# Gated delta rule in one encoder layer: state updates of the two directions as neighbouring 64-row products

## The chip, the cores and the metric

The kernel runs on one core of one Trainium2 chip. The metric is the device time of one execution in microseconds (us); of several runs the median is given. Engines are named as in the profile: PE is TensorE (PEld its weight loads), DVE is VectorE, ACT is ScalarE, POOL is GpSimd, SP is SyncE, which here only issues DMAs. PSUM is the memory into which TensorE writes; it is divided into 8 banks of 512 fp32 numbers per partition.

## The reference

One layer of a bidirectional encoder over 1024 tokens of width 1024: one input projection feeds neighbourhood attention (8 heads of 64) and a gated DeltaNet (4 heads of 128, both directions), then come an output projection and a hierarchical mixture of experts. The change touches the DeltaNet's recurrence alone. Per head and direction it goes over 16 chunks of 64 tokens:

```
def step(state, inp):
    q_c, k_c, u_c, w_c, g_c, qk_c = inp
    v_new = u_c - einsum('bhck,bhkv->bhcv', w_c, state)
    o_c = (einsum('bhck,bhkv->bhcv', q_c * exp(g_c)[..., None], state)
           + einsum('bhij,bhjv->bhiv', qk_c, v_new))
    g_last = g_c[..., -1:]
    state = (state * exp(g_last)[..., None]
             + einsum('bhck,bhcv->bhkv', k_c * exp(g_last - g_c)[..., None], v_new))
    return state, o_c
```

The state is 128 x 128 per head and direction. The second direction goes over the tokens from the end.

## The kernel before

All of it is one function, `tile_layer`. Its parts in time: the projections for the DeltaNet with their convolutions and decays (to about 217 us), the inversion of the chunks' triangular matrices (lines 443 to 493, to about 351 us), the recurrence (lines 498 to 571, 360 to 513 us), the attention (from line 596), output projection and router, and the experts (from 780 us), whose weights come from HBM.

**Recurrence.** The two directions of a chunk are handled together: direction 0 has partitions 0 to 63 (`hf[0]`), direction 1 has 64 to 127 (`hf[1]`); `DH` is 4 heads, `DD` is 128, `CH` is 64, `NCH` is 16. For each chunk n:

- SP issues eight DMAs (lines 516 to 520) for the inverted matrix and the attention matrix of the chunk (`at`, block-diagonal over the two directions, zeroed once at line 507), for v (`vn`) and for k (`kn`). GpSimd scales k into `kd` (line 522).
- Line 531: TensorE multiplies k and q of the chunk (`qkT`, 128 columns: 64 of k, 64 of q) with the state, per head and direction, into the bank `pk0` or `pk1`. Lines 533: VectorE reads the k half of it into `r`, 64 rows at a time.
- Line 537: per head, one product over all 128 partitions gives the new values of both directions in the bank `pw`.
- Lines 539 and 540: after each pair of heads ScalarE copies the rows of direction 0 and VectorE those of direction 1 into `w`, in which each direction has its own 128 columns and the rest is zero (memset once at line 508, two buffers). Line 542: ScalarE copies `pw` once more as a whole into `wc`.
- Line 548: per head, one product of `kd` (all 128 partitions) with `w` (256 columns) gives the updates of both directions side by side, in the bank `ps0` for heads 0 and 1 and `ps2` for heads 2 and 3. GpSimd scales the old state (line 552), VectorE adds (line 555): `sn`, the next chunk's `st`.
- Line 560: ScalarE scales the q half of `pk` into `o`, 64 rows at a time. Line 563: per head, one product of `at` with `wc` goes into the bank of `pw`; VectorE adds it (line 567), and GpSimd issues two DMAs to `on_d` (line 569).

An fp32 product stands in the trace as two records, each with its own weight load. Each of the tiles pk0, pk1, pw, ps0 and ps2 has one bank and one buffer; three more banks (`psF`) hold the projections' results.

**What fills the gaps.** The projections of z, v, k and q of the attention (`nat_block`, lines 575 to 587; eight blocks of 192 products of 256 columns, fp32r, through `mm3` on lines 84 to 86, tile `pA`) stand behind the recurrence in the program. Each product in `mm3` is three: high parts, and high with low parts in both ways. Line 417 transposes their results on TensorE, lines 424 and 428 write k and q to DRAM (`kk_d`, `q_d`). Seven blocks are free to run beside the recurrence, and the last is mixed with the first attention steps (lines 681 to 690).

**Order.** The program is a sequence of instructions; when it is built, a scheduler puts them in an order for each engine by their places in the program and by its own estimates of times, and adds the waits. It lets two accesses to one PSUM bank not overlap, where one is a write or where two engines read. On the chip each engine then keeps its order. After the recurrence `scn.close()` and `lng.close()` (lines 592 and 593) give its memory back, and the attention's tiles are allocated in it: `vw` (line 601), loaded by 16 DMAs on SP (line 605), and the buffers for q and k (`q2`, `k2`, `kl`), loaded by DMAs that GpSimd issues (lines 620 to 622) and read on lines 639 and 640.

Of the kernel before, what the change touches and what calls it, by code (L numbers as in the profile page):

```python
# [8 lines left out]
F32 = mybir.dt.float32  # L9
# [3 lines left out]
AF = mybir.ActivationFunctionType  # L13
OP = mybir.AluOpType
# [5 lines left out]
P = 128  # L20
# [5 lines left out]
DH, DD = 4, 128  # L26
# [10 lines left out]
def tile_layer(ctx, tc, a, out):  # L37
    nc = tc.nc
    pe, act, dve, pool, sp = nc.tensor, nc.scalar, nc.vector, nc.gpsimd, nc.sync
# [24 lines left out]
    qkT = dnp.tile([P, DH, NCH, 2 * CH], F32, name="qkT")  # L64
# [110 lines left out]
    step = lambda d, n: n if d == 0 else NCH - 1 - n  # L175
    gt = dnp.tile([P, 10, NCH, DH], F32, name="gt")
    X, T1, T2, BETA, G, GC, EGC, DL, C1, C2 = (gt[:, i] for i in range(10))
    egl = dnp.tile([P, 2, NCH, DH], F32, name="egl")
# [285 lines left out]
    with tc.tile_pool(name="ty", bufs=1, side="right") as ty:  # L464
# [13 lines left out]
        for g in range(4):  # L478
            ms = range(g * 16, g * 16 + 16)
            gs = slice(g * 16, g * 16 + 16)  # L480
            pw = psB.tile([P, 16, 32], F32, name="pB")
# [17 lines left out]
    sc1 = scn.enter_context(tc.tile_pool(name="sc1", bufs=1, side="right"))  # L499
    sc2 = scn.enter_context(tc.tile_pool(name="sc2", bufs=2, side="right"))  # L500
    psK = scn.enter_context(tc.tile_pool(name="psK", bufs=1, space=PSUM, side="right"))
    hf = [slice(d * 64, d * 64 + 64) for d in range(2)]

    atb = [sc1.tile([P, 2, DH, 2, CH], F32, name=f"at{i}") for i in range(2)]
    wb = [sc1.tile([P, DH, 2, DD], F32, name=f"w{i}") for i in range(2)]
    for i in range(2):
        pool.memset(atb[i], 0.0)
        pool.memset(wb[i], 0.0)
    st = None
    for n in range(NCH):  # L510
        ch = [slice(step(d, n) * CH, step(d, n) * CH + CH) for d in range(2)]
        kn = sc2.tile([P, DH, DD], F32, name="kn")
        vn = sc2.tile([P, DH, DD], F32, name="vn")
        at, w = atb[n % 2], wb[n % 2]
        for d in range(2):
            sp.dma_start(at[hf[d], 1, :, d], T_d[hf[d], n])
            sp.dma_start(vn[hf[d]], v_d[ch[d]])
        for d in range(2):
            sp.dma_start(kn[hf[d]], k_d[ch[d]])
            sp.dma_start(at[hf[d], 0, :, d], SA_d[hf[d], n, :, 1])  # L520
        kd = sc2.tile([P, DH, DD], F32, name="kd")
        pool.tensor_tensor(kd, kn, DL[:, n, :, None].to_broadcast([P, DH, DD]), op=OP.mult)
        if n == 0:
            r = vn
        else:
            r = sc2.tile([P, DH, DD], F32, name="r")

            pk = [psK.tile([P, DH, DD], F32, name=f"pk{d}") for d in range(2)]
            for h in range(DH):
                for d in range(2):  # L530
                    pe.matmul(pk[d][:, h], qkT[:, h, step(d, n)], st[:, h, d], start=True, stop=True)
                for d in range(2):
                    dve.scalar_tensor_tensor(r[hf[d], h], pk[d][hf[0], h], nE[hf[d], n, h:h + 1], vn[hf[d], h],
                                             op0=OP.mult, op1=OP.add)
        pw = psK.tile([P, DH, DD], F32, name="pw")
        for h in range(DH):
            pe.matmul(pw[:, h], at[:, 1, h], r[:, h], start=True, stop=True)
            if h % 2 == 1:
                act.activation(w[hf[0], h - 1:h + 1, 0], pw[hf[0], h - 1:h + 1], AF.Copy)
                dve.tensor_copy(w[hf[1], h - 1:h + 1, 1], pw[hf[1], h - 1:h + 1])  # L540
        wc = sc2.tile([P, DH, DD], F32, name="wc")
        act.activation(wc, pw, AF.Copy)
        if n < NCH - 1:
            sn = sc2.tile([P, DH, 2, DD], F32, name="sn")
            for g in range(0, DH, 2):
                ps = psK.tile([P, 2, 2, DD], F32, name=f"ps{g}")
                for h in range(g, g + 2):
                    pe.matmul(ps[:, h - g], kd[:, h], w[:, h], start=True, stop=True)
                if n == 0:
                    dve.tensor_copy(sn[:, g:g + 2], ps)  # L550
                else:
                    pool.tensor_tensor(sn[:, g:g + 2], st[:, g:g + 2],
                                       egl[:, :, n, g:g + 2].rearrange("p d h -> p h d")[:, :, :, None].to_broadcast([P, 2, 2, DD]),
                                       op=OP.mult)
                    dve.tensor_tensor(sn[:, g:g + 2], ps, sn[:, g:g + 2], op=OP.add)
        o = sc2.tile([P, DH, DD], F32, name="o")
        if n > 0:
            for h in range(DH):
                for d in range(2):
                    act.activation(o[hf[d], h], pk[d][hf[1], h], AF.Copy, scale=EGC[hf[d], n, h:h + 1])  # L560
        po = psK.tile([P, DH, DD], F32, name="pw")
        for h in range(DH):
            pe.matmul(po[:, h], at[:, 0, h].rearrange("p d c -> p (d c)"), wc[:, h], start=True, stop=True)
        if n == 0:
            dve.tensor_copy(o, po)
        else:
            dve.tensor_tensor(o, po, o, op=OP.add)
        for d in range(2):
            pool.dma_start(on_d[d, ch[d]], o[hf[d]].rearrange("p h e -> p (h e)"))
        if n < NCH - 1:  # L570
            st = sn
# [362 lines left out]
    for i in range(done, nb + 3):  # L934
# [11 lines left out]
        if i >= nb // 2 + 7 and i % 2 == 0 and not (tail[0][0] is ao_pre and tail[0][1] == 4):  # L946
            f, t = tail.pop(0)
# [6 lines left out]
    def load_w(mw, e, eng=sp, after=None, how=mybir.DependencyClass.Sync, parts=(0, 1)):  # L954
        ws = []
        for i in parts:
            w = mw.tile([P, 2048], F32, name="wd") if i else mw.tile([P, 2, 2048], F32, name="wg")
            ins = eng.dma_start(w, a[("w_gu", "w_down")[i]][e])
            if after is not None:
                tc.add_manual_dep(ins.ins, after.ins.name, mybir.DependencyInfo(how, mybir.DependencyReason.DATA),  # L960
                                  reason="more urgent transfers first")
            ws.append(w)
        return ws
# [181 lines left out]
    for i in range(NS):  # L1145
        gp, e = steps[i]
        args = (pool, ins, mybir.DependencyClass.NoSync) if i == 0 else ()
        for n, part in upto(i):
            f = steps[n // 2][1]
# [20 lines left out]
    with tc.If(rest > 0):  # L1170
        with tc.For_i(0, 64) as e:
            left = nc.values_load(ci[:, bass.ds(e + 64, 1)], min_val=0, max_val=14)
            with tc.For_i(0, left) as i:
                w = load_w(mwA, e)
# [71 lines left out]
```

## Time and profile before

| | us |
|---|---|
| median of 3 runs | 1406.26 |
| lowest and highest | 1401.35 and 1408.34 |
| the profiled execution | 1408.78 |
| its span, first to last instruction | 1407.0 |
| PE busy | 1194.1 (85%) |
| DVE busy | 660.1 (47%) |
| ACT busy | 393.9 (28%) |
| POOL busy | 387.4 (28%) |

The rows below come from the profiled execution, with times from the start of its span. Busy time counts an engine while an instruction of its own runs. Matmuls are pipelined, and their ends are modelled, so a row of PE is better read by its starts: the distance from one start to the next. Idle time of an engine is put down to what released it, as the semaphores tell. The granted clock is a share of TensorE's full 2.4 GHz. The DMA share is the mean busy share of the core's 16 DMA engines, as the packets' times sum up, and can exceed 1.

### The profile page before, as it was taken

To read this page: it belongs to the slowest core of one execution; us is meant where nothing else is said; L and a number is where in the kernel's file an instruction comes from. 1 tells how busy PE (TensorE), PEld (TensorE's weight loads), DVE (VectorE), ACT (ScalarE), POOL (GpSimd) and SP (SyncE) were. 2 spreads that over 40 slices of the span, in tenths; PEclk is the share of its full clock that TensorE was granted. 3 is DMA by queue.
4 is the path that set the end of the run, shared out by engine and by line. 5 is a ranking of instruction groups with operands and counts; after the bars stand their busy time and mean duration, and the time that the engine had idled before them with its cause. 6 is when DMAs were issued, how large, how long until landed. Compare 5 with 4: busy or idle time off the path is not lost. (4 is left out here: it accounts for less than half of the span.)

```text
span 1407.0 us, 20840 instructions
## 1 busy us (share of the span) xinstructions
PE 1194.1 (85%) x7307; PEld 828.0 (59%) x7308; DVE 660.1 (47%) x1631; ACT 393.9 (28%) x800; POOL 387.4 (28%) x435
## 2 busy tenths in 40 slices
PE   6977999979999996688989968888887788878885
PEld 6866889969988895466768853333332333333332
DVE  5556853853667652667858871212211212222211
ACT  6435422322354441765445320000000000000000
POOL 1147313021655544112110242212212112211111
PEclk9989999989999997799999979999998899989998
DMA  4251246346565469998694788999999899998991
GB/s 158 71 114 42 75 135 177 94 138 148 166 176 148 119 172 221 297 262 206 169 216 165 285 332 323 397 404 401 400 406 394 352 387 407 395 364 331 402 379 38
DMA packets 109953, 347.11 MB, mean 247 GB/s; under 512 B 43104, under 2 KB 49248, under 8 KB 93168
## 3 DMA queue, kind: packets, MB, share of 16 engines
q1 hardware_dynamic: 74480, 260.68, 51.3%
q0 software_dynamic: 27056, 68.79, 19.0%
q10 hardware_dynamic: 8272, 15.78, 3.2%
q8 instruction: 82, 1.34, 0.4%
q14 instruction: 63, 0.52, 0.1%
HBM read 305.26 MB, written 61.67 MB: 261 GB/s over the span
## 5 line engine op out<-in xcount | busy, mean ns | idle before, releaser
L1041 PE MATMUL pp<-wg,xT 128*64 128x512 f32 x1024 | 233.1, 604 | 19.7 <-DVE xT L1030 19.4
L1041 PEld LDWEIGHTS pp<-wg,xT 128*64 128x64 f32 x1024 | 74.4, 139 | 156.4 <-issue 128.2
L1076 PE MATMUL po<-wd,hT 128*64 128x512 f32 x512 | 126.8, 622 | 45.1 <-DVEq L1155 28.3
L84 PE MATMUL pA<-w_hi,h_hi 128*128 128x256 f32 x512 | 151.1, 295 | 0.0
L86 PE MATMUL pA<-w_hi,h_lo 128*128 128x256 f32 x512 | 149.9, 293 | 0.0
L85 PE MATMUL pA<-w_lo,h_hi 128*128 128x256 f32 x512 | 149.9, 293 | 0.0
L1057 POOL DMA_INDIRECT out<-yg,tS x32 | 50.8, 1587 | 291.3 <-DVE yg L1078 242.8
L1045 DVE SCALAR_TENSOR_TENSOR sg<-pp,tS,sg 128x256 f32<-128x256 f32 x32 | 15.5, 484 | 233.2 <-ACTq L1155 189.0
L1076 PEld LDWEIGHTS po<-wd,hT 128*64 128x64 f32 x512 | 42.1, 142 | 129.5 <-issue 68.4
L1078 DVE TENSOR_SCALAR yg<-po,tS 128x512 f32<-128x512 f32 x64 | 47.0, 749 | 126.2 <-DMA out<-yg,tS 66.8
L84 PEld LDWEIGHTS pA<-w_hi,h_hi 128*128 128x128 f32 x512 | 100.5, 196 | 0.7 <-issue 0.2
L85 PEld LDWEIGHTS pA<-w_lo,h_hi 128*128 128x128 f32 x512 | 100.4, 196 | 0.2
L86 PEld LDWEIGHTS pA<-w_hi,h_lo 128*128 128x128 f32 x512 | 100.2, 196 | 0.3
L1044 ACT ACTIVATE sg<-pp,tS 128x256 f32<-128x256 f32 x32 | 15.2, 474 | 272.7 <-PE pp L1041 272.7
L84 PE MATMUL pA<-h_hi,w_hi 128*128 128x512 f32 x192 | 76.5, 398 | 0.0
L85 PE MATMUL pA<-h_lo,w_hi 128*128 128x512 f32 x192 | 76.4, 398 | 0.0
L86 PE MATMUL pA<-h_hi,w_lo 128*128 128x512 f32 x192 | 75.9, 395 | 0.0
L76 DVE TENSOR_TENSOR w_lo<-w_raw,w_hi 128x512 fp32r<-128x512 f32 x56 | 38.5, 702 | 71.1 <-ACT w_hi L75 69.4
L250 DVE SCALAR_TENSOR_TENSOR acc<-raw,convw,acc 128x1024 f32<-128x1024 f32 x48 | 63.2, 1320 | 12.4 <-ACT acc L248 11.9
L1053 ACT ACTIVATE hT<-ph 128x256 f32<-128x256 f32 x32 | 12.3, 384 | 191.6 <-PE ph L1051 191.6
L84 PE MATMUL pA<-wo_hi,t_hi 128*128 128x512 f32 x128 | 54.7, 427 | 9.3 <-ACT t_hi L750 6.9
L665 PE MATMUL pv<-pT,vw 128*128 128x256 f32 x192 | 55.2, 425 | 3.3 <-ACT pT L656 2.2
(340 smaller groups left out, 2422.4 us busy)
## 6 DMA issues: line engine op xcount, KB each, us to landing
wg<-in_w_gu SPq DMA_DIRECT2D x62, 2048.0 KB
wd<-in_w_down SPq DMA_DIRECT2D x63, 1024.0 KB
bt<-in_bias SPq DMA_DIRECT2D x24, 384.0 KB
w_raw<-in_w_nat SPq DMA_DIRECT2D x32, 256.0 KB
w_raw<-in_w_dn SPq DMA_DIRECT2D x24, 256.0 KB
k<-kk_d POOLq DMA_DIRECT2D x16, 384.0 KB
SA_d<-cm POOLq DMA_DIRECT2D x8, 512.0 KB
kk_d<-ev POOLq DMA_DIRECT2D x8, 512.0 KB
```

What stands on the lines that cost most here:

```text
L76: dve.tensor_sub(lo[:, k:k + 2], raw, hi[:, k:k + 2].bitcast(F32))
L84: pe.matmul(dst, sh, mh, start=(i == 0), stop=False)
L85: pe.matmul(dst, sh, ml, start=False, stop=False)
L86: pe.matmul(dst, sl, mh, start=False, stop=(i == n - 1))
L250: dve.scalar_tensor_tensor(acc, raw[:, t:t + S], convw[:, m, t:t + 1], acc, op0=OP.mult, op1=OP.add)
L665: pe.matmul(pv, vw[:, w, half + g, pr * P:(pr + 1) * P], pT[:, g], start=(g == 0), stop=(g == 2))
L1041: pe.matmul(pp[d * CAP:(d + 1) * CAP], xT[:, k, d * CAP:(d + 1) * CAP], ws[d][0][:, :, k * 256:(k + 1) * 256], start=(k == 0), stop=(k == ...
L1044: act.activation(sg[:n], pp[:n, 0], AF.Silu, scale=mf[:n, 3:4])
L1045: dve.scalar_tensor_tensor(sg[:n], pp[:n, 1], mf[:n, 3:4], sg[:n], op0=OP.mult, op1=OP.mult)
L1057: ins = pool.indirect_dma_start(out=out, out_offset=bass.IndirectOffsetOnAxis(ap=idx, axis=0), in_=yg, in_offset=None, bounds_check=S - 1, ...
L1076: pe.matmul(po[d * CAP:(d + 1) * CAP], hT[:, k, d * CAP:(d + 1) * CAP], w[1][:, k * D + c * 512:k * D + (c + 1) * 512], start=(k == 0), st ...
L1078: dve.tensor_scalar(yg[:n, cs], po[:n], mf[:n, 2:3], None, op0=OP.mult)
```

## The change

It has four parts. `w` with its zeros and its memsets goes; `pw` is copied once into `wc`, heads 0 and 1 by ScalarE and heads 2 and 3 by VectorE, after all four products. The state products are one per head and direction, over the 64 partitions of that direction, into a bank per direction; neighbours in the program are the two directions of a head. State, update and scaling are laid out by direction first, so an add takes all heads of one direction. And pk is made for all heads of direction 0, then of direction 1, each followed by VectorE's four reads.

```diff
     atb = [sc1.tile([P, 2, DH, 2, CH], F32, name=f"at{i}") for i in range(2)]
-    wb = [sc1.tile([P, DH, 2, DD], F32, name=f"w{i}") for i in range(2)]
     for i in range(2):
         pool.memset(atb[i], 0.0)
-        pool.memset(wb[i], 0.0)
...
-            for h in range(DH):
-                for d in range(2):
-                    pe.matmul(pk[d][:, h], qkT[:, h, step(d, n)], st[:, h, d], start=True, stop=True)
-                for d in range(2):
+            for d in range(2):
+                for h in range(DH):
+                    pe.matmul(pk[d][:, h], qkT[:, h, step(d, n)], st[:, d, h], start=True, stop=True)
+                for h in range(DH):
                     dve.scalar_tensor_tensor(r[hf[d], h], pk[d][hf[0], h], nE[hf[d], n, h:h + 1], vn[hf[d], h],
                                              op0=OP.mult, op1=OP.add)
         pw = psK.tile([P, DH, DD], F32, name="pw")
+        wc = sc2.tile([P, DH, DD], F32, name="wc")
         for h in range(DH):
             pe.matmul(pw[:, h], at[:, 1, h], r[:, h], start=True, stop=True)
-            if h % 2 == 1:
-                act.activation(w[hf[0], h - 1:h + 1, 0], pw[hf[0], h - 1:h + 1], AF.Copy)
-                dve.tensor_copy(w[hf[1], h - 1:h + 1, 1], pw[hf[1], h - 1:h + 1])
-        wc = sc2.tile([P, DH, DD], F32, name="wc")
-        act.activation(wc, pw, AF.Copy)
+        act.activation(wc[:, 0:2], pw[:, 0:2], AF.Copy)
+        dve.tensor_copy(wc[:, 2:4], pw[:, 2:4])
         if n < NCH - 1:
-            sn = sc2.tile([P, DH, 2, DD], F32, name="sn")
-            for g in range(0, DH, 2):
-                ps = psK.tile([P, 2, 2, DD], F32, name=f"ps{g}")
-                for h in range(g, g + 2):
-                    pe.matmul(ps[:, h - g], kd[:, h], w[:, h], start=True, stop=True)
+            sn = sc2.tile([P, 2, DH, DD], F32, name="sn")
+
+            ps = [psK.tile([P, DH, DD], F32, name=f"ps{d}") for d in range(2)]
+            for h in range(DH):
+                for d in range(2):
+                    pe.matmul(ps[d][:, h], kd[hf[d], h], wc[hf[d], h], start=True, stop=True)
+            for d in range(2):
                 if n == 0:
-                    dve.tensor_copy(sn[:, g:g + 2], ps)
+                    dve.tensor_copy(sn[:, d], ps[d])
                 else:
-                    pool.tensor_tensor(sn[:, g:g + 2], st[:, g:g + 2],
-                                       egl[:, :, n, g:g + 2].rearrange("p d h -> p h d")[:, :, :, None].to_broadcast([P, 2, 2, DD]),
-                                       op=OP.mult)
-                    dve.tensor_tensor(sn[:, g:g + 2], ps, sn[:, g:g + 2], op=OP.add)
+                    pool.tensor_tensor(sn[:, d], st[:, d], egl[:, d, n, :, None].to_broadcast([P, DH, DD]), op=OP.mult)
+                    dve.tensor_tensor(sn[:, d], ps[d], sn[:, d], op=OP.add)
```

## Rows read from the trace of the kernel before

**Rows 1.** Busy us by stretch: PE, PEld, DVE, ACT, POOL; clock, DMA share, GB/s.

```profile
366.00:512.00 146.00, 136.15 (x953) 121.25 (x953) 100.27 (x226) 69.92 (x184) 78.95 (x87) 1.00 0.53 141
...
512.00:537.00 25.00, 24.29 (x203) 23.96 (x203) 9.33 (x17) 5.01 (x9) 16.56 (x18) 1.00 1.09 281
```

**Rows 2.** Groups by line, 360 to 510 us: busy us, mean ns | idle before, releasers.

```profile
L533 DVE SCALAR_TENSOR_TENSOR r<-pk,nE,vn 64x128 f32<-64x128 f32 x120 | 41.2, 343 | 9.5 <-PE pk L531 7.0
L560 ACT ACTIVATE o<-pk,gt 64x128 f32<-64x128 f32 x117 | 37.8, 360 | 16.8 <-DVE r L533 14.9 <-ACT w L539 0.8
L86 PE MATMUL pA<-w_hi,h_lo 128*128 128x256 f32 x115 | 35.4, 308 | 0.0
...
L548 PE MATMUL ps<-w,kd 128*128 128x256 f32 x120 | 33.5, 385 | 0.5 <-DVE w L540 0.2
...
L555 DVE TENSOR_TENSOR sn<-ps,sn 128x512 f32<-128x512 f32 x28 | 19.3, 691 | 14.4 <-PE ps L548 12.8 <-PE pA L417 1.4
...
L539 ACT ACTIVATE w<-pw 64x256 f32<-64x256 f32 x32 | 12.1, 377 | 51.2 <-PE pw L537 45.4 <-DVE qn L406 5.5
```

**Rows 3.** TensorE in order of time, one chunk: start, duration, line, tiles, records.

```profile
374.30 1.03 PE L548 MATMUL ps<-w,kd 128*128 128x256 f32 x4
375.17 1.05 PE L563 MATMUL pw<-wc,at 128*128 128x128 f32 x8
376.06 0.61 PE L531 MATMUL pk<-sn,qkT 128*128 128x128 f32 x4
...
376.62 0.28 PE L85 MATMUL pA<-w_lo,h_hi 128*128 128x256 f32 x1
376.74 0.28 PE L86 MATMUL pA<-w_hi,h_lo 128*128 128x256 f32 x1
```

**Rows 4.** TensorE in order of time: products on two column halves (128*64) of the array.

```profile
211.70 1.03 PE L261 MATMUL pB<-ident,acc 128*128 128x128 f32 x8
212.67 3.71 PE L342 MATMUL pB<-qkT 128*64 128x128 f32 x64
216.31 0.38 PE L84 MATMUL pA<-w_hi,h_hi 128*128 128x256 f32 x1
```

**Rows 5.** TensorE in order of time: 32 x 32 products on different rows and columns.

```profile
349.24 0.19 PE L490 MATMUL pB<-TT,wt 32*32 32x32 f32 x1
349.25 0.19 PE L489 MATMUL pB<-TT,wt 32*32 32x32 f32 x1
349.27 0.19 PE L490 MATMUL pB<-TT,wt 32*32 32x32 f32 x1
```

**Rows 6.** Waits from 366 to 512 us: who for whom, us in total, times, longest.

```profile
PEld pk L531 <- DVE r L533: 7.5, 9, 1.4
DVE w L540 <- ACT w L539: 7.3, 6, 1.7
...
PE pk L531 <- DVE r L533: 5.6, 7, 1.2
```

**Rows 7.** All engines in order of time: from a chunk's first pk to the next.

```profile
401.64 0.68 PE L531 MATMUL pk<-sn,qkT 128*128 128x128 f32 x4
...
409.06 0.72 DVE L533 SCALAR_TENSOR_TENSOR r<-pk,nE,vn 64x128 f32<-64x128 f32 x2
...
411.52 0.43 DVE L540 COPY w<-pw 64x256 f32<-64x256 f32 x1
...
412.35 0.49 PE L531 MATMUL pk<-sn,qkT 128*128 128x128 f32 x2 [0.52 <-ACT o L560]
```

**Rows 8.** Line 508's memsets: count, duration ns min/median/max, first and last start.

```profile
L508 POOL MEMSET w<- x2: 963/970/976, 355.9 to 357.7; 128x1024 f32 x2
```

**Rows 9.** SP's issues for vw; TensorE's first attention products, with their waits.

```profile
510.48 13.30 SPq L605 DMA_DIRECT2D vw<-av_d x16
...
541.34 0.66 PE L639 MATMUL pq<-k,q 128*128 128x384 f32 x1 [4.26 <-DMA k<-kk_d]
543.60 0.66 PE L640 MATMUL pq<-kl,q 128*128 128x384 f32 x1 [1.60 <-DMA kl<-kk_d]
```

More of the change, by code (lines that the diff above doesn't have):

```diff
@@ L513, in tile_layer @@
         vn = sc2.tile([P, DH, DD], F32, name="vn")
-        at, w = atb[n % 2], wb[n % 2]
+        at = atb[n % 2]
         for d in range(2):
```

## Prediction, made before the change was built

> **What bounds the kernel now.** I read the busy time by stretch first, then the groups by line in the stretch of the recurrence, then TensorE's order in time, then the waits. The recurrence runs from 366 to 512 us: 15 chunks after the first, 9.7 us each. In it TensorE is busy 136 of 146 us at the full granted clock (1.00 in the row), VectorE 100, ScalarE 70; from 512 to 537 TensorE is busy 24.3 of 25 [rows 1]. TensorE has two kinds of work there [rows 2]: the products of the recurrence (fp32; each shows as two records) and the projection products pA (fp32r, 3 lines of 115 records), which fill the gaps; what of them doesn't fit follows until 537. So any TensorE time freed between 366 and 537 should bring the end of the projections forward, and a shorter chain of chunks alone only moves pA from inside the recurrence to behind it.
>
> How full TensorE is, its starts show better than its busy time [rows 3]: the 4 records of L548 (256 columns) take 374.30 to 375.17, 0.217 us each; the 8 of L563 (128 columns) 375.17 to 376.06, 0.111 each; pA 0.12 each. Per chunk that is 16 x 0.111 for pk, 8 x 0.111 for pw, 8 x 0.217 for the state products, 8 x 0.111 for po, and 23 x 0.12 for pA: 1.8 + 0.9 + 1.7 + 0.9 + 2.8 = 8.1 of 9.7 us. The 1.6 us that are left are waits, 24 us over 15 chunks.
>
> **The state products.** Now 4 fp32 products per chunk, 128 rows by 256 columns, half of them zeros of w: 15 x 8 x 0.217 = 26.0 us. After: 8 products of 64 rows by 128 columns, the two directions of a head next to each other on different rows of the array and in different banks. If neighbours run at the same time, the nearest rows give the price: L342, fp32 on two halves of the array, has 64 records of 128 columns from 212.67 to 216.31, 0.057 each, where L261 on the whole array takes about 0.11 [rows 4]. Then 15 x 16 x 0.057 = 13.7 us, a gain of 12.3. But L342's halves are columns of the array; a pair on different rows is only seen with 32 x 32 products, which start 0.01 us apart and come at about 0.015 us a record [rows 5]. If neighbours don't overlap, the cost is 15 x 16 x 0.111 = 26.6, a loss of 0.6. A gain beyond 12.3 is excluded: there are only two halves. I take 12.3, since L342 has the very columns and type.
>
> Going between the whole array and halves has a price. L261's 8 records should end at 211.70 + 0.89 = 212.59, and L342 starts at 212.67: 0.08 us on the way in [rows 4]. The way out I can't separate, and set equal. The two copies of pw end one after the other, so the products come in two visits a chunk: 0.2 x 2 x 15 = 6 us at most, 0 at least (one visit that coincides with a wait). I take 6. By this row the products give 12.3 - 6 = 6.3 us net.
>
> The Trainium skill speaks here against the change: TensorEngine Tiling (Array Packing), Key Properties, says that changing the tiling mode (not just the tile) drains TensorE. By that rule, with an estimate of a drain as an L548 record's duration less its pitch (0.385 less 0.217 [rows 2, 3]), two visits of two edges would cost 10 us over 15 chunks and leave 2. The trace agrees that there is a cost, but its one edge has 0.08.
>
> **The order of pk.** Now each head's two products are followed by VectorE's two reads of the same banks (0.34 us each [rows 2]), and the next head's products wait for them: 7.5 us on the weight queue, 5.6 on TensorE [rows 6]. After, four products of direction 0 run, then four of direction 1 while VectorE reads the first bank. Most of these 13.1 us should go, but something is late next: the first pk of a chunk needs the old pk read out by ScalarE's 8 scalings (0.36 us each [rows 2]; the wait at 412.35 is for them [rows 7]), and pw needs VectorE's last reads. Bounds: 13 gained, 3 lost if the new single wait is longer than the four old ones. I take 4, nearer the small end, since TensorE's order is fixed at build time and fill placed by a plan doesn't move into a wait.
>
> **Copies, adds, scalings.** Per chunk ScalarE loses one 64-row copy (0.38) and half of the whole-bank copy, VectorE one copy of 0.43 [rows 2, 7]. ScalarE and VectorE have idle time for it [rows 1], so as work this is worth nothing; if ScalarE's cover failed it would be its 0.38 a chunk. On the path the two copies still stand one behind the other (VectorE's waits on ScalarE's, 7.3 us [rows 6], although they read other partitions of the bank), 0.8 us now and then. The adds (0.69 [rows 2]) and GpSimd's scalings keep count and size: 0. The two memsets of w go, 0.97 each on GpSimd ahead of the first chunk [rows 8]; bound 0 to 1.9 us gained, taken as 0, since the first chunk also needs its DMAs. GpSimd's later instructions and the DMA issues on SP keep their places: no DMA is added or moved.
>
> **Behind the recurrence.** The attention's buffers reuse the recurrence's memory, so the 16 loads of vw are issued only from 510.48 us, over 13.3 us; DMA is then at 1.09 of its 16 engines [rows 1, 9]. In that crowd TensorE waits 4.26 us for k and 1.60 for kl [rows 9]. If the recurrence ends earlier than the projections do, these loads are out of the way. Bounds 0 to 5.9 gained; I take 4.
>
> **The sum.** 12.3 - 6 + 4 + 0 + 4 = 14.3 us. The profiled execution took 1408.8 us (span 1407.0 and 1.8 around it): 1394.5. It was 2.5 above the median of the runs shown (1406.26), so against the median 1392.0. What comes behind (attention, experts) starts on what was computed before it, so I let the gain pass through whole.
>
> **Rivals.**
> *No gain that shows.* A record of 128 stationary columns never came faster than 0.111 us [rows 3]; L342's 0.057 has 64 stationary columns [rows 4]. So it may be the weights that set the pitch, and the change has twice as many loads of 128 columns. Then the products lose 0.6 and the switches 6, against 4 and 0 to 4 gained: 0 to 3 us off, 1403 to 1409. The same follows if other work gets between the neighbours in TensorE's order. For it: the two rows can't be told apart. Against: the 32 x 32 pairs, at 0.015 a record [rows 5]. The Trainium skill has the rule, in TensorE: Matmul & The Clock Gate, LDWEIGHTS: the time of a load goes with its columns and not with its rows. No run here shows a 64-row load of 128 columns.
>
> *A larger gain.* In one chunk the first pk starts at 401.64, VectorE's last two reads end at 409.78, and the next chunk's first pk at 412.35 [rows 7]: the reads take 8.2 us of 10.7. In the new order eight reads (2.7) follow four products (0.9): near 4. The chunk could fall to some 7.5 us and the recurrence end by 480. TensorE's sum still holds, so the gain is 12.3 with switches hidden in waits, plus 11 of the 13.1 us of waits, plus 5 of DMA waits: 28 us, 1378. Against it: pA's products stand between in a fixed order, and much of the 8.2 us is pA.
>
> *Slower.* Now the first pair of heads is copied, multiplied and added while the second pair is still read; after, everything waits for the last pw, and the first pk of the next chunk stands behind pw 0.45 (two records and a tail), copies 0.38 and 0.43, products 0.6 to 1.0 and an add 0.69: 2.6 to 3.0 us, with some 0.05 at each of five hand-overs near 3.3, against 2.57 now (409.78 to 412.35) [rows 7]. If the reads keep their 8.2 us because fill stands between them, each chunk is 0.7 us longer: 15 x 0.7 = 10.5, 1417 from the median. It decides as soon as the reads take over 7.5 us.
>
> **How the numbers follow.** Forecast 0.42 (own range 1385 to 1399), larger gain 0.18, no gain 0.26, slower 0.14. Half a per cent, 7 us, is about what a measurement of this kernel can tell from no change. The first two are faster by more: 0.60; same 0.26; slower 0.14. The range for 8 in 10 leaves out most of the slower case and the far end of the larger gain: 1374 to 1411.
>
> **What would show it.** Right: the new L548 line with 240 records whose neighbours start within 0.02 us and come at 0.06 a record; the waits of pk for r nearly gone; the recurrence shorter than 140 us; TensorE's waits for k and kl under 3 us. Wrong: state records at 0.11 us, or single visits with 0.2 us around each; a longer chunk with TensorE waiting at the first pk or at pw; or a recurrence that is shorter by 10 us and more while attention starts at the same time, which would mean that something other than TensorE sets the start of attention.

## The result, and the profile after

The changed kernel takes **1387.21 us** (median of 4 runs, 1385.71 to 1392.52), where the kernel before, timed beside it, took 1407.3: a ratio of 0.9869, 95% interval [0.9842, 0.9895], 20 us less. The prediction was 1392.0, with a range of 1374 to 1411, and faster. A second measurement of the changed kernel, among the experiments, gave 1386.0 and 0.986 [0.9843, 0.9878].

Where the time went shows in four starts that every trace has: the first pk of the recurrence, the first product of the last projection block (`nat_block` number 8), VectorE's first logits, the last value product of the attention. The table gives the first, then the stretches between them, for all the kernels that follow (one profiled execution each; the two of the changed kernel show how far such numbers move by themselves).

| kernel | first pk at | to the last projection block | to the first logits | to the last values | to the end | span |
|---|---|---|---|---|---|---|
| before | 366.1 | 152.2 | 42.6 | 216.6 | 629.5 | 1407.0 |
| after | 366.0 | 138.9 | 41.2 | 215.1 | 625.2 | 1386.4 |
| after, second profile | 362.8 | 135.3 | 41.3 | 212.6 | 629.2 | 1381.2 |
| pk's order alone | 368.0 | 147.7 | 41.1 | 215.5 | 627.5 | 1399.8 |
| all but pk's order | 365.3 | 146.2 | 40.7 | 217.1 | 630.8 | 1400.1 |
| products not neighbours | 369.1 | 141.4 | 35.2 | 214.6 | 628.1 | 1388.4 |
| products on 128 rows | 368.3 | 140.6 | 40.1 | 211.5 | 630.6 | 1391.1 |
| copies back | 368.1 | 138.3 | 38.7 | 208.8 | 627.9 | 1381.8 |
| vw later | 363.8 | 135.0 | 22.4 | 223.3 | 626.7 | 1371.2 |
| vw later, second profile | 367.3 | 135.8 | 22.7 | 223.9 | 627.3 | 1377.0 |
| vw later, not neighbours | 368.2 | 139.1 | 24.6 | 227.7 | 628.8 | 1388.4 |
| vw and q, k, kl later | 368.6 | 136.3 | 22.4 | 225.7 | 628.1 | 1381.1 |
| vw in two parts | 368.7 | 136.6 | 22.7 | 228.6 | 625.1 | 1381.7 |
| a quarter of vw | 367.7 | 135.5 | 20.4 | 219.3 | 629.9 | 1372.8 |

Of the 20.6 us between the spans of before and after, 13.3 lie in the first stretch; of the 25.8 to the second profile, 16.9.

The busy time by stretch of the changed kernel (columns as in [rows 1]) covers the recurrence, which now ends at 486 us instead of 513, what follows of the projections, and the pause before the attention:

```profile
360.00:487.00 127.00, 114.63 (x1014) 108.71 (x1013) 85.69 (x212) 53.72 (x156) 74.19 (x84) 0.96 0.60 159
487.00:525.00 38.00, 36.43 (x303) 35.88 (x301) 12.88 (x24) 6.91 (x12) 21.46 (x23) 1.00 1.13 272
525.00:547.00 22.00, 11.32 (x65) 10.74 (x66) 7.32 (x23) 2.55 (x4) 10.80 (x15) 0.69 0.61 132
```

TensorE is still nearly full up to 525. But the projections that no longer fit into the shorter recurrence now run beside the DMAs, whose share rises to 1.13, and from 525 TensorE is idle half the time.

The groups by line, 360 to 500 us (columns as in [rows 2]):

```profile
L545 PE MATMUL ps<-wc,kd 64*128 64x128 f32 x240 | 18.2, 287 | 6.4 <-ACT wc L537 3.2 <-DVE wc L538 2.4 <-POOL kd L520 0.7
L529 PE MATMUL pk<-sn,qkT 128*128 128x128 f32 x240 | 32.8, 295 | 5.4 <-DVE sn L551 5.4
L531 DVE SCALAR_TENSOR_TENSOR r<-pk,nE,vn 64x128 f32<-64x128 f32 x120 | 33.7, 340 | 4.0 <-PE pk L529 2.7
```

L545 holds the new state products: 18.2 us busy instead of 33.5 for L548 [rows 2], by starts 19.6 instead of 26.7. VectorE's reads of pk (L531) keep their 340 ns, but are busy 33.7 instead of 41.2 in sum [rows 2], since eight in a row overlap. In the waits, 360 to 500 us (columns as in [rows 6]), pk no longer waits for r; it waits for the new state, and the state products for the copies:

```profile
DVE wc L538 <- ACT wc L537: 14.2, 12, 2.2
...
PEld pk L529 <- DVE sn L551: 6.3, 4, 3.5
PE pk L529 <- DVE sn L551: 5.4, 4, 3.2
...
PE ps L545 <- ACT wc L537: 3.2, 2, 2.2
PE ps L545 <- DVE wc L538: 2.4, 2, 1.5
```

One chunk, all engines in order of time (start, duration, engine, line):

```profile
424.53 1.95 PE L529 MATMUL pk<-sn,qkT 128*128 128x128 f32 x16
...
425.63 2.28 DVE L531 SCALAR_TENSOR_TENSOR r<-pk,nE,vn 64x128 f32<-64x128 f32 x8
...
428.69 0.38 ACT L537 ACTIVATE wc<-pw 128x256 f32<-128x256 f32 x1
...
429.11 0.42 DVE L538 COPY wc<-pw 128x256 f32<-128x256 f32 x1 [1.20 <-ACT wc L537]
429.22 1.16 PE L545 MATMUL ps<-wc,kd 64*128 64x128 f32 x16
...
430.31 1.16 PE L559 MATMUL pw<-wc,at 128*128 128x128 f32 x8
430.49 1.29 DVE L551 TENSOR_TENSOR sn<-ps,sn 128x512 f32<-128x512 f32 x2 [0.95 <-PE ps L545]
...
431.31 1.98 PE L529 MATMUL pk<-sn,qkT 128*128 128x128 f32 x16
```

From pk to pk it is 6.8 us (10.7 in the chunk of [rows 7]; over all chunks some 8.0 instead of 9.7). All 16 records of the state products go in one visit, a stay of TensorE on one kind of product, of 1.09 us. In single starts the two directions of a head begin 6 to 7 ns apart here (up to 36 in other visits), a pair comes every 0.112, 0.056 a record, and the last one is 0.202 before the next line's, where records on the whole array are 0.111 apart.

### The profile page after: what moved, and what is told of

It reads as the page before. It is cut to its first block, busy times and chain, and to the rows that moved or that the text cites. A ratio compares the mean times of both kernels' runs of the same rounds, so it can differ in the third digit from the quotient of the medians.

```text
span 1386.4 us, 21032 instructions
## 1 busy us (share of the span) xinstructions
PE 1177.5 (85%) x7427; PEld 821.7 (59%) x7428; DVE 643.5 (46%) x1615; ACT 375.8 (27%) x768; POOL 381.9 (28%) x433
## 5 line engine op out<-in xcount | busy, mean ns | idle before, releaser
L1037 PE MATMUL pp<-wg,xT 128*64 128x512 f32 x1024 | 229.7, 598 | 17.7 <-DVE xT L1026 16.7
L85 PE MATMUL pA<-w_lo,h_hi 128*128 128x256 f32 x512 | 148.9, 291 | 0.0
L85 PEld LDWEIGHTS pA<-w_lo,h_hi 128*128 128x128 f32 x512 | 100.9, 197 | 0.0
L85 PE MATMUL pA<-h_lo,w_hi 128*128 128x512 f32 x192 | 76.6, 399 | 0.0
L250 DVE SCALAR_TENSOR_TENSOR acc<-raw,convw,acc 128x1024 f32<-128x1024 f32 x48 | 63.2, 1319 | 11.5 <-ACT acc L248 11.1
L1049 ACT ACTIVATE hT<-ph 128x256 f32<-128x256 f32 x32 | 12.3, 384 | 193.4 <-PE ph L1047 193.4
```

Of the source, the lines that this page charges most:

```text
L85: pe.matmul(dst, sh, ml, start=False, stop=False)
L250: dve.scalar_tensor_tensor(acc, raw[:, t:t + S], convw[:, m, t:t + 1], acc, op0=OP.mult, op1=OP.add)
L1037: pe.matmul(pp[d * CAP:(d + 1) * CAP], xT[:, k, d * CAP:(d + 1) * CAP], ws[d][0][:, :, k * 256:(k + 1) * 256], start=(k == 0), stop=(k == ...
```

## The experiments

### pk's order, alone and taken back

The kernel before with the new order of pk alone, and the changed kernel with the old order:

```diff
-            for h in range(DH):
-                for d in range(2):
+            for d in range(2):
+                for h in range(DH):
                     pe.matmul(pk[d][:, h], ...
```

> The kernel before, with the new order of pk alone (four products of direction 0, VectorE's four reads, then direction 1); w, its copies and the 256-column state products stay. Theory: the waits for r go (13 us), the chunk falls from 9.7 to 8.5 to 9.0, the time is 1394 to 1401. Rival 'order alone': 1385 to 1391. Rival 'pairs alone': 1403 to 1409.

> The changed kernel, with pk's order back: per head both directions, then VectorE's two reads. Theory (the pairs save TensorE time and the order of pk shortens the chunk, both count): the state products still take about 1.0 us a chunk for 16 records, TensorE's waits for r come back (10 us and more), a chunk is 8.8 to 9.3 us, the time 1394 to 1400. Rival 'order alone': 1402 to 1409, as before the change. Rival 'pairs alone': 1385 to 1390, as with the whole change.

Measured: alone 1399.37 (1397.8 to 1401.5), 0.9953 [0.9934, 0.9971]; taken back 1397.05 (1395.1 to 1401.8), 0.9935 [0.9917, 0.9953]. So the order is worth some 6.5 us by itself and 10 on top of the products. The groups of pk's products, first in the kernel before with the new order:

```profile
L531 PE MATMUL pk<-sn,qkT 128*128 128x128 f32 x240 | 29.3, 275 | 0.0
```

then in the changed kernel with the old order (224 of the 240 records lie in the rows' window):

```profile
L529 PE MATMUL pk<-sn,qkT 128*128 128x128 f32 x224 | 46.2, 296 | 7.8 <-DVE r L531 3.9 <-DVE sn L551 3.8
```

In the old order each head's results must be read before the next head may write, so the 240 records stand in 119 short rows with fill between them; in the new one they stand in 15 rows of 16. The busy sums, 46.2 against 29.3 to 32.8, make too much of that: the last record of each row counts its whole 0.275 us, though the next product starts 0.03 to 0.11 behind it, so each further row adds to the sum without costing that time. The starts are safer. From the start before to its own, pk's 240 records take 47.9 us in the old order, 9.9 of them idle, and 36.4 in the changed kernel, 5.4 idle. So of the 11.5 us between them 4.5 show as idle; the other 7 are switches between fill and pk and short waits, which the profile counts as busy. A part of it comes back in the fill; the first stretch of the table is 7.3 us shorter. In the kernel before the new order takes pk from 45.0 us to 26.8, but TensorE's idle time ahead of pw and the state products rises from 0.8 to 11.6 us: most of the wait moves to the next step, and 4.5 us are left in the stretch.

### The products: apart, and on all rows

In the changed kernel, first the four products of direction 0, then those of direction 1:

```diff
-            for h in range(DH):
-                for d in range(2):
+            for d in range(2):
+                for h in range(DH):
                     pe.matmul(ps[d][:, h], kd[hf[d], h], wc[hf[d], h], start=True, stop=True)
```

> The changed kernel, with the eight state products ordered by direction: four of direction 0, then four of direction 1, so that neighbours stand on the same rows. Theory: the 16 records come at 0.11 us, 1.8 us a chunk in place of 1.0, which is on the chunk's path and on TensorE: 0.75 x 15 = 11 us more at most, 1394 to 1399. Rival 'order alone' (the pairing is worth nothing): 1385 to 1390. Rival 'pairs alone': 1403 and more.

And each product over 128 rows, which adds up the updates of both directions in each:

```diff
-                    pe.matmul(ps[d][:, h], kd[hf[d], h], wc[hf[d], h], start=True, stop=True)
+                    pe.matmul(ps[d][:, h], kd[:, h], wc[:, h], start=True, stop=True)
```

> The changed kernel, with the eight state products over all 128 partitions (kd[:, h], wc[:, h]), so that both banks get the sum of both directions' updates: same count, columns, banks and order, no halves of the array and no change of its division. Theory: 16 records at 0.11 us as without neighbours, but no 0.1 to 0.2 us at the edges: 1391 to 1398. If the edges cost nothing, the same as with the products ordered by direction; if they are a drain of 0.2 us each, 3 to 6 us less than that.

TensorE in order of time, products apart:

```profile
433.47 1.71 PE L545 MATMUL ps<-wc,kd 64*128 64x128 f32 x16
435.11 1.16 PE L559 MATMUL pw<-wc,at 128*128 128x128 f32 x8
```

and on 128 rows:

```profile
432.27 2.02 PE L545 MATMUL ps<-wc,kd 128*128 128x128 f32 x16
434.13 1.06 PE L559 MATMUL pw<-wc,at 128*128 128x128 f32 x8
```

The visit takes 1.64 us apart and 1.86 on 128 rows, against 1.09 as neighbours: the pairing is worth 0.55 us a chunk. Apart, the records of one direction come at 0.112, as those of 128 rows do; around the change of direction three pairs start 4 to 6 ns apart. So the 16 starts take 1.44 us, against 1.75 on 128 rows and 0.89 as neighbours.

The way out of the 64-row products costs 0.19 us more than on 128 rows: the first record of the next line comes 0.202 behind the last of theirs (0.112 on 128 rows), and its second another 0.213 behind (0.112). The rows of L559 above show the second part, 1.16 long and 1.06. The way in costs 0.08 where nothing else holds the visit: in the three visits behind a product of L85 it is 0.21 on 64 rows and 0.13 on 128. In the others both start 0.19 or more behind the last projection product, on 128 rows as soon as the copy is released.

The whole time is another matter. Apart: 1386.96 (1385.0 to 1390.2), 0.9864 [0.9844, 0.9884], the same as the changed kernel, where 1394 to 1399 was expected. On 128 rows: 1392.42 (1390.7 to 1394.9), 0.9908 [0.9888, 0.9928]. The table shows where the first loses the difference: the last projection block begins later (141.4 us after the first pk, against 135.3 and 138.9), and then 35.2 instead of 41 us pass to the first logits. What the pairing wins, the stretch before the attention takes back; with the loads of vw later, below, it shows.

### Two copies back

A ScalarE copy of the whole bank and a VectorE copy of half of it, into a tile that nobody reads:

```diff
         dve.tensor_copy(wc[:, 2:4], pw[:, 2:4])
+        wx = sc2.tile([P, DH, DD], F32, name="wx")
+        act.activation(wx, pw, AF.Copy)
+        dve.tensor_copy(wx[:, 2:4], pw[:, 2:4])
```

> The changed kernel with two copies more per chunk, into a tile that nobody reads: the whole bank by ScalarE (0.6 us) and half of it by VectorE (0.42), about what the change took off these engines. The prediction gave the copies as work no price: within 2 us of the changed kernel, chunk unchanged at 6.8 us. Rival (the copies are a part of the gain, since ScalarE's scalings, which free pk, stand behind them): a chunk 0.4 to 1.0 us longer, 1391 to 1398.

1384.98 (1382.8 to 1389.2), 0.9869 [0.9832, 0.9907]: nothing. As work the copies have no price: 16.2 us of work came in, beside TensorE's (groups by line, 360 to 500 us):

```profile
L540 ACT ACTIVATE wx<-pw 128x512 f32<-128x512 f32 x16 | 9.5, 596 | 1.4 <-DVE wc L538 1.1
L541 DVE COPY wx<-pw 128x256 f32<-128x256 f32 x16 | 6.7, 422 | 7.6 <-ACT wx L540 7.6
```

But no product reads `wx`. In the kernel before, the product behind the state products (L563) read what ScalarE's second copy wrote, and waited for it (columns as in [rows 6]):

```profile
PEld pw L563 <- ACT wc L542: 5.2, 10, 0.9
...
PE pw L563 <- ACT wc L542: 2.0, 6, 0.6
```

TensorE's 2.0 us of this are gone in the changed kernel. This run doesn't bring them back, and no other shows what they are worth in the whole time.

### What holds the stretch before the attention

In the changed kernel SP issues the loads of vw as soon as the recurrence's memory is free, and ScalarE, which splits the projections' k and q into `ev` (L421), must wait for an earlier `ev` to reach DRAM. SP's issues:

```profile
486.73 13.20 SPq L601 DMA_DIRECT2D vw<-av_d  x16
```

ScalarE in order of time:

```profile
513.65 0.69 ACT L421 ACTIVATE ev<-pA,qkg 128x512 fp32r<-128x512 f32 x1 [2.13 <-DMA kk_d<-ev]
...
523.40 0.69 ACT L421 ACTIVATE ev<-pA,qkg 128x512 fp32r<-128x512 f32 x1 [5.69 <-DMA kk_d<-ev]
```

and TensorE's pauses. The first stands behind that wait; the second is the chain of the block's last tile through ScalarE, VectorE and GpSimd, in which no wait for a DMA shows:

```profile
527.63 1.09 PE L417 MATMUL pA<-ident,qn 128*128 128x128 f32 x4 [3.37 <-DVE qn L406]
...
543.55 1.11 PE L417 MATMUL pA<-ident,qn 128*128 128x128 f32 x4 [5.92 <-DVE qn L406]
```

After the first pause TensorE's granted clock is 0.50, the lower of its two levels (1.2 GHz), for five us:

```profile
524.00:528.00 4.00, 0.63 (x5) 0.46 (x4) 2.03 (x4) 0.69 (x2) 2.89 (x3) 0.79 0.99 234
528.00:533.00 5.00, 5.00 (x23) 5.00 (x22) 0.91 (x3) 0.69 (x1) 1.97 (x3) 0.50 0.88 186
```

Columns as in [rows 1]. Four versions put transfers later; all are the changed kernel otherwise. The loads of vw wait for the last product of projection block 7:

```diff
+        for tp, _ in enumerate(nat_block(bi)):
+            if (bi, tp) == (6, 3):
+                mark = marks[tp]
...
-            sp.dma_start(vw[r * 32:(r + 1) * 32, w], src)
+            ld = sp.dma_start(vw[r * 32:(r + 1) * 32, w], src)
+            tc.add_manual_dep(ld.ins, mark.ins.name, ..., reason="later")
```

> The changed kernel, with one more wait: the 16 loads of vw wait for the last product of the seventh projection block (about 504 us), in place of the end of the recurrence (486). Theory now (behind the recurrence not TensorE binds but the ev buffers, whose writes to kk_d and q_d crawl among vw's loads): the wait of TensorE for qn near 527 us (3.4 us) goes, the first logits come 2 to 5 us earlier, 1382 to 1386. Rival (the crowd moves with the loads, or vw is then late for its first use at 552 us): 1387 to 1394, with a new wait at the first product with vw. Rival (TensorE's order alone sets the start of attention): within 2 us of the changed kernel.

The same with the products apart:

> Both edits: state products ordered by direction, so that neighbours share rows, and vw's loads behind the seventh block. If the pairs' 0.5 us a chunk was hidden by the DMA crowd, it shows once the crowd is gone: 4 to 7 us slower than with the loads later alone. If it is hidden by something else (the last block's own chain), the two are within 2 us.

vw later, and the loads of q, k and kl issued 4 steps ahead instead of 8; and with the second half of vw behind the first logits besides:

> The changed kernel with vw's loads behind the seventh projection block, and the loads of q, k and kl issued four attention steps later than now (four steps ahead of their use in place of eight). Theory (DMA binds from the end of the recurrence to some 560 us; with vw later alone, TensorE stood idle 17.8 us at 556 us because those loads and the output projection's weights crowded the first tile's): the stall falls by 5 us and more, 1366 to 1374. Rival (q and k are then late themselves): a new wait at the logits, 1376 to 1386.

> As the one before, with only the first half of vw (two of four column windows) loaded behind the seventh block and the second half behind the first logits. Theory: 2 MB leave the stretch before the first logits and move to where they are used: logits 2 to 5 us earlier, the sum 1364 to 1373. Rival (DMA is full throughout, so the order of the loads only moves the wait): within 3 us of the one before.

The changed kernel again, beside these:

> The changed kernel itself, on the same chip as the other two, to compare them with: 1383 to 1391.

| kernel | us | ratio |
|---|---|---|
| vw later | 1377.84 (1372.8 to 1384.6) | 0.9826 [0.9786, 0.9866] |
| vw later, products apart | 1388.48 (1385.0 to 1390.1) | 0.9877 [0.9843, 0.9912] |
| vw and q, k, kl later | 1382.74 (1379.7 to 1386.3) | 0.9838 [0.9817, 0.9859] |
| vw in two parts | 1385.09 (1383.4 to 1385.5) | 0.9851 [0.9836, 0.9866] |
| the changed kernel again | 1386.0 (1382.8 to 1386.8) | 0.986 [0.9843, 0.9878] |

With vw later the first logits come 22 to 25 us after the last projection block begins, not 41. But from there the attention takes 8 to 16 us longer. Moving q, k and kl too, or vw in two parts, was expected to bring the time to 1374 and less and did not; the second came within 3 us of the first, as its rival had it. With the products as neighbours vw alone seemed to keep a gain, over a wide spread. With the products apart it keeps none: 9 to 11 us lie between 1388.48 and the two measurements with neighbours (1377.84, and 1379.47 below), where 4 to 7 were expected. So with the loads later the pairing shows in the whole time, though 0.55 us a chunk make only 8, and 3 to 4 of them lie in the first stretch of the table. The last two runs ask for the cause (a quarter of vw: one window of four is loaded and used for all, so the values of three windows are left out) and for the gain:

```diff
-    for w in range(4):
+    for w in range(1):
...
-            pe.matmul(pv, vw[:, w, half + g, pr * P:(pr + 1) * P], ...
+            pe.matmul(pv, vw[:, 0, half + g, pr * P:(pr + 1) * P], ...
```

> The changed kernel with one of the four windows of vw loaded (1 MB of 4) and used for all four windows, so that the values of three windows are left out. Theory, that the DMA engines set the stretch between the recurrence and the first logits: from the first product of the last projection block to the first logits 30 us or less (about 41 in the changed kernel), and a time 8 to 15 us under the changed kernel's 1386, 1371 to 1378. Rival, that the order of the transfers only moves a wait, or that something else sets the stretch: the stretch within 4 us of 41, the time within 3 us of 1386.

> The kernel with the loads of vw behind the last projection block, a second time, with more rounds. If what it gained over the changed kernel (1377.8 against 1386 to 1387) was the order of the loads: 1375 to 1382. If it was the early execution that it happened to have and the wait for the first output tile takes the gain back: 1384 to 1388.

A quarter of vw: 1371.33 (1363.68 to 1375.94), 0.9754 [0.9728, 0.9779], and 20.4 us to the first logits. TensorE, in the busy time by stretch, has no pause there:

```profile
503.00:523.00 20.00, 20.00 (x169) 20.00 (x167) 7.08 (x14) 4.71 (x8) 10.73 (x12) 1.00 0.95 200
```

So 15 us in the end time come and go with 3 MB of loads. That the transfers alone set the stretch isn't shown, though, because the edit also changed the order of VectorE's work, which the scheduler makes anew. In the changed kernel the first logits stand on VectorE behind the last tile of the projections, with no wait of their own, while TensorE made their products 17 us earlier:

```profile
528.37 0.67 PE L635 MATMUL pq<-k,q 128*128 128x384 f32 x1
...
545.42 0.75 DVE L422 SCALAR_TENSOR_TENSOR ev<-pA,qkg,ev 128x512 f32<-128x512 f32 x1 [1.93 <-ACT ev L421]
546.09 0.55 DVE L639 CUSTOM_DVE_ANT_0 lg<-pq,bt 128x384 f32<-128x384 f32 x1
```

With a quarter of vw they stand ahead of that tile:

```profile
521.79 0.42 PE L635 MATMUL pq<-k,q 128*128 128x384 f32 x1
...
523.59 0.55 DVE L639 CUSTOM_DVE_ANT_0 lg<-pq,bt 128x384 f32<-128x384 f32 x1
```

The four versions with later loads have this order too (22 to 25 us in the table), all others the former (35 to 43). To the end of the last block's products it is 32.1 us in the changed kernel and 25.4 with a quarter of vw: these 6.7 us hold the pause, the lower clock and the waits for transfers. The other 14 of the 21 go with the order. No run changes the order without the loads.

vw later, again: **1379.47** (1378.1 to 1380.31), 0.982 [0.9802, 0.9837]. Its interval ends below both of the changed kernel's. The later loads, with the order that comes with them, are worth some 7 us, and this is the fastest of the versions that compute the whole layer. Why it isn't 18, as the stretch before the logits says, its trace shows. Busy time by stretch:

```profile
503.00:526.00 23.00, 22.11 (x185) 21.94 (x184) 7.95 (x16) 4.91 (x8) 10.64 (x12) 1.00 1.18 262
540.00:560.00 20.00, 2.47 (x12) 1.43 (x10) 5.75 (x13) 5.49 (x9) 4.46 (x7) 0.70 1.08 255
```

and TensorE in order of time:

```profile
561.41 1.00 PE L747 MATMUL pA<-ident,ot 128*128 128x128 f32 x3 [18.22 <-DVE ot L740]
```

TensorE now stands still for 18.22 us before the first tile of the output (`ot`, loaded from `on_d`), where it waited 0.47 in the changed kernel. The DMA share is 1.08, and for 9.2 us of that time VectorE waits for the other half of the tile (`ob`) to land: what was won before the logits is lost to transfers at another place.

## Why the prediction was right

The direction and the main terms were right; that the sum came near owes something to luck, since terms that were too large and one that was too small cancel.

**State products, predicted 12.3 - 6.** The pitch was right: 0.056 a record, where L342's column halves had 0.057 [rows 4]. That does away with the "no gain" rival: a load of 64 rows takes as long as one of 128 (0.188 us and 0.192), but the loads for the two halves run at the same time. A visit's price was about right too, 0.2 predicted, 0.19 out and up to 0.08 in measured; but there is one visit a chunk, not two: 2.9 to 4 us, not 6. The Trainium skill's rule (TensorEngine Tiling (Array Packing), Key Properties), that a change of tiling mode drains TensorE, agrees with this trace: the 0.19 on the way out is near the estimate of 0.17 for an edge, and the 10 us in all counted twice as many edges. What the prediction left out are waits for the copies: 3.2 us inside the visits, nearly all in two of them, and 3.2 ahead of the last two visits. From the first record of each visit to the next line's, L548 took 26.7 us in all and L545 takes 19.6: 7.1. Less 1.5 for the next line's late second record that makes 5.6, where 6.3 was predicted, before the waits ahead of the visits.

**pk's order, predicted 4.** This is the term that was mis-sized: 6.5 alone, 10 with the rest. The prediction took the small end "since TensorE's order is fixed at build time and fill placed by a plan doesn't move into a wait". But the plan was made anew: the fill now lies behind the row of 16 records. The bound of 13 was misread besides: the 7.5 us of the weight queue and the 5.6 of TensorE [rows 6] are the same waits, seen by two queues of one engine, and all 5.6 lie inside the 7.5. Something was late next, as was said: 5.4 us of TensorE's waits for the new state. That the term gained more than TensorE's 5.6 lies in switches and short waits that don't show as idle, by the starts 7 us of pk's 11.5.

**Copies, 0.** As work right: two copies put back cost nothing. That TensorE waited 2.0 us for the second copy was overlooked.

**Behind the recurrence, predicted 4.** 1.4 (42.6 to 41.2 us in the table). TensorE no longer waits for k and kl, as predicted, but the reason given, that the loads of vw would be out of the way, was wrong. They are issued 24 us earlier (486.73 instead of 510.48) and projections that no longer fit into the recurrence run behind it, so the crowd of transfers meets the last projection blocks instead of the first logits: 5.69 us of ScalarE's wait for `kk_d`, and behind it 3.37 of TensorE's for `qn`.

**The sum.** These pieces overlap and can't be added. The runs split the gain so: everything but pk's order is worth 8.9 (1405.9 to 1397.05), where the prediction had 10.3, and pk's order 10 on top, where it had 4. What of the 8.9 is pairing, copies or layout isn't settled: without the pairing alone the whole time stays the same, and with the loads of vw later it is 9 to 11 us longer.

**The rivals.** The *larger gain* had the chunk right, 7.5 (6.8 undisturbed), and the end of the recurrence, 480 (486), but its 28 us counted waits for DMA as gone and pk's waits twice. *Slower* needed reads of more than 7.5 us: from the chunk's first pk at 424.53 to the copy at 428.69 it is 4.2. Of what would have shown the forecast wrong, the last came half true: something other than TensorE does set the start of the attention (the place of the first logits on VectorE, behind the last tile), but it moved along by 14.8 us (560.9 to 546.1).

## What to carry to other kernels

Products that use half of the array's rows gain in full only when their partner on the other half is the next instruction (here in a bank of its own; one bank for both wasn't tried). Order them by pair, keep them in one visit, and look at starts, since durations say nearly the same paired or not. A line's busy sum counts the tail of each short row of products, over which the next product already runs: take the distances between starts before crediting a change with busy time. Waits of TensorE and of its weight queue are often one wait; don't add them. When a stage is made shorter, look at the transfers that its end lets go. And when an edit moves loads, compare every engine's order before and after: the scheduler may have moved other work too, as it did here with the first logits.

## What the runs showed of the hardware that was not expected

Two fp32 streams on the two row halves of the array run at the full rate of each: a record every 0.112 us on either half, as on all rows, so 16 records of 128 columns with 16 weight loads of their own have starts over 0.89 us, against 1.75 on all rows. Leaving that mode cost 0.19 us in each of 15 visits, half of it ahead of the next line's first product and half ahead of its second. Entering it cost 0.08 in three visits; in the others a wait hid all or part of it.
